# A gated backbone layer on one core: fp32 state products become three fp32r passes, norm weights move into later copies, and the order of tasks changes

## The chip, the cores and the metric

The kernel runs on one core of one Trainium2 chip. The metric is the device time of one execution of the program on that core, in microseconds, and the median over the runs counts.

## The reference, cut to what matters

One layer, 1024 latent tokens behind 256 context tokens, width 1024. One input projection feeds two branches: a bidirectional chunked gated linear attention (GLA, 4 heads, keys of 128, values of 256) and a differential attention (8 heads, values of 128). Each branch is normalised, weighted per channel, gated, projected; the two are merged by gates and projected once more.

```python
h  = modulate(x, shift, scale); hc = modulate(ctx, ...)      # RMSNorm, adaLN
gq, gk, gv, gg, lr, dq, dk, dv, dg, mg, md = split(h @ w_in) # and of hc
# GLA, per head and direction; cum is the running sum of log_a in a chunk
scores  = (q * exp(cum - ref)) @ (k * exp(ref - cum)).T
o_intra = tril(scores) @ v
k_state = k * exp(last - cum)
s = decay * s + k_state.T @ v             # the state, chunk after chunk
o = o_intra + (q * exp(cum)) @ s          # forward plus backward
# differential attention, per head
a = softmax(q1 @ k1.T) - lam * softmax(q2 @ k2.T);  od = a @ vd
# merge
A = rms_norm(o)  * gla_norm                  * silu(gg)
B = rms_norm(od) * diff_norm * (1 - lam_init) * silu(dg)
y = sigmoid(mg) * (A @ w_br_gla) + sigmoid(md) * (B @ w_br_diff)
out = x + g_x * (y @ w_out)
```

All inputs and outputs are float32. `gla_norm` has 256 entries, one per value channel of a head, and `diff_norm` has 128.

## The kernel before, in words

**How it is written.** A scheduler in the program (`Driver`) writes out the instruction streams of all engines. Each piece of work is a Python generator, a task, started by `spawn(task, at, prio)`. The scheduler keeps its own clock, which follows TensorE's planned time, and of the tasks that are due it lets the one with the smallest `prio` number issue its next instructions. A task gives way with `yield`: for an event, for a planned time, or with `yield d.on("ACT", *tiles)` until the planned time at which the tiles are ready and ACT's planned queue has room. `acq(tag)` waits for a buffer of a pool and `rel(tag, at)` gives it back. So priorities, events and pool sizes set the order in which instructions stand on each engine. Once written, each engine runs its stream in order, and a semaphore wait of one instruction holds everything behind it on that engine. Most engine instructions go through one helper and carry line L201; matrix multiplications carry L349, transposes L375. In the profile they are told apart by the names of their tiles.

**Two kinds of matmul.** `mm` on float32 operands is one fp32 instruction, which leaves two records in the profile. `mm3` takes operands split into an upper half `hi` and a remainder `lo`, both of type fp32r, and adds up three fp32r matmuls: hi x hi, hi x lo, lo x hi. `split` makes the two halves: ACT copies to `hi`, and DVE subtracts `hi` from the source to give `lo`.

**The stages, in order of time.**

- 0 to 80 us: the prologue. The adaLN vectors, the normalised tokens, transposed into the blocks `hk` (context) and the `h` tiles, and the low-rank decay inputs.
- 80 to 176 us: the projections `gk` and `gq`. Within them `job_la` computes the log decays `g` for all heads on ACT (Exp, then Ln, which need another activation table) and stores them; `job_gate` makes sums of tokens (`gb` steps on DVE).
- 176 to 519 us: four pairs of projections, each 1024 channels, by a scheme with seven products (`BY7`, in the order `gv`, `dv`, `dg`, `gg`). Sums of weights are formed ahead (`sums`), stored to `d_s` and read back. `gv` are the GLA values, stored to `d_v` as float32; `dv` the values of the attention, stored to `d_dv` as two halves; `dg` and `gg` are the two gates, finished as SiLU by `post_gate` or `direct`, which end with a multiplication on POOL by the norm weights (`gdif`, 128x512, or `ggla`).
- 520 to 910 us: the remaining projections (keys and queries of the attention, merge gates) on TensorE, and between their matmuls the four GLA heads.
- 910 to 1455 us: the attention, 64 units of 128 queries of one head, with the projection by `w_br_gla` (`mb`) as filler between its matmuls. `att_order` lists the turns: scores `S`, transposes `T`, at @ values `A`. `AHEAD0` units of scores come first, and then scores run `LEAD` units ahead.
- To 1626 us: the projection by `w_br_diff`, the merge, the output projection.

**One GLA head** (function `gla`). `prep` loads keys and decays and forms their running sums. `kstates(0)` and `kstates(1)`, for the two directions, go through five groups of two 128-token blocks: load the values `gv` by DMA, exponential `ge` on ACT, product with the keys on POOL, two transposes on TensorE into the psum tile `gt`, copy to `gkt` on ACT. `products` multiplies `gkt` by `gv`, two fp32 matmuls per group into psum `gt`, and `upd` on DVE adds them to the decayed state: `gsb` in `bwd`, `gsf` in `fstates`. `intra` forms the scores from factors of queries and keys, masks them on POOL (`gsc`) and adds the two directions on DVE (`gso`). `forward` adds up, per group, six matmuls into psum `go`: for each of the two blocks, queries by forward state, queries by backward state, scores by values. `post` normalises, multiplies by the gate and transposes (`tp<-ident,gp`); ACT and DVE split the transposed result into two halves `pl`, which are stored to `d_aT`. In the attention, `att_fin` transposes likewise (`b1`), and ACT copies the result to `bb`, which is stored to `d_bT`.

The line that starts a direction's group of products, and the one that adds scores by values:

```python
en = self.mm(pu[:, j], kt[:, j], v[:, j], True, True)        # products
en = self.mm(po[:, j], sc[:, j], v[:, j], False, True)       # forward
```

Of the kernel before, what the change touches and what calls it, by code (L numbers as in the profile page):

```python
# [232 lines left out]
class Hybrid:  # L233
# [10 lines left out]
        gk=("sbA2", 1), gla=("sbA2", 2), gq=("sbA2", 1), gsb=("sbA2", 8), gsf=("sbA2", 4), ge=("sbA2", 2),  # L244
        gkt0=("sbA2", 2), gkt1=("sbA2", 2), gqe=("sbA2", 4), gqr=("sbA2", 1), gkk=("sbA2", 1),
        gsc=("sbA2", 1), gso=("sbA2", 2), gp=("sbA2", 2), gj=("sbA2", 1), gv0=("sbA2", 2), gv1=("sbA2", 2),
# [157 lines left out]
    def scratch(self):  # L404
# [4 lines left out]
        self.d_v = [d(f"d_v{c}", [T, 512]) for c in range(2)]  # L409
# [46 lines left out]
    def consts_late(self):  # L456
# [9 lines left out]
        self.ggla = self.c("ggla", [P, 256])  # L466
        self.dma(self.ggla, bc(a["gla_norm"][0], 256))
        self.gdif = self.c("gdif", [P, P])
        self.dma(self.gdif, bc(a["diff_norm"][0], P))
# [10 lines left out]
        self.pool.tensor_scalar(self.ggla, self.ggla, 0.5, 0.0, ALU.mult, ALU.add)  # L480
        self.pool.tensor_scalar(self.gdif, self.gdif, 1.0 - LAM_INIT, 0.5, ALU.mult, ALU.mult)
# [348 lines left out]
    def phase_a(self):  # L830
# [8 lines left out]
        self.gla_done, self.gla_free, self.gla_back, self.gla_intra, self.gla_sf = (  # L839
            [Event() for _ in range(4)] for _ in range(5))  # L840
# [29 lines left out]
        self.ev_pl, self.ev_pw, self.ev_zl = Event(), Event(), Event()  # L870
# [36 lines left out]
    BY7 = (("gv", C_GV), ("dv", C_DV), ("dg", C_DG), ("gg", C_GG))  # L907
# [35 lines left out]
    def pair_weights(self, cols, ev_load, ev_run):  # L943
# [54 lines left out]
        def run():  # L998
            yield ev_run
            for g in range(len(cols)):  # L1000
# [23 lines left out]
                for n, o in (("t1", "w22"), ("t3", "w12"), ("t4", "w21"), ("v22", "v22")):  # L1024
                    for k in range(4):
# [71 lines left out]
    def pairs(self, wp):  # L1097
# [3 lines left out]
        def loads():  # L1101
# [7 lines left out]
            for g, (what, _) in enumerate(self.BY7):  # L1109
                w = 512 if what in ("dg", "gg") else 640  # L1110
                for n in self.SUMS:
                    for k in range(4):
# [5 lines left out]
                        d.set(ev_z[g, n, k], d.when(z))  # L1118
                        if (g, n, k) == (len(self.BY7) - 1, "s4", 1):
                            d.set(self.ev_zl)  # L1120
# [27 lines left out]
        for g, (what, _) in enumerate(self.BY7):  # L1148
# [5 lines left out]
            def out(g, r, c, t, x, tag):  # L1154
# [3 lines left out]
                if what in ("dg", "gg"):  # L1158
# [6 lines left out]
                    yield e  # L1165
                    gain, dst, w = (self.gdif, self.d_dg, P) if what == "dg" else (self.ggla, self.d_gg, 256)
# [1635 lines left out]
```

## Time and profile before

| what | value |
|---|---|
| median of 3 runs | 1622.63 us (1622.59 to 1624.02) |
| time of the profiled execution | 1627.62 us |
| its span; mean granted TensorE clock | 1625.9 us; 0.996 |
| TensorE matmul / weight load (PE / PEld) busy | 98% / 82% |
| VectorE (DVE) / ScalarE (ACT) / GpSimd (POOL) busy | 75% / 51% / 39% |
| moved by DMA | 331.16 MB, mean 204 GB/s |

How to read the views: a group of instructions has a line number, an engine, an operation and its tiles as output<-inputs, a shape and a count, then busy time and mean duration, then the idle time in front of them and what ended it. "128x512" is partitions by elements. The chain that ended last is followed backwards from the last instruction; a matmul counts in it only until the next one takes over. The windows view gives for a stretch of time each engine's busy time, and behind them the granted clock as a share of full speed, the share of time that the DMA engines were busy, and GB/s.

### The profile page before, as it was taken

To read this page: it belongs to the slowest core of one execution; us is meant where nothing else is said; L and a number is where in the kernel's file an instruction comes from. 1 tells how busy PE (TensorE), PEld (TensorE's weight loads), DVE (VectorE), ACT (ScalarE), POOL (GpSimd) and SP (SyncE) were. 2 spreads that over 40 slices of the span, in tenths; PEclk is the share of its full clock that TensorE was granted. 3 is DMA by queue.
4 is the path that set the end of the run, shared out by engine and by line. 5 is a ranking of instruction groups with operands and counts; after the bars stand their busy time and mean duration, and the time that the engine had idled before them with its cause. 6 is when DMAs were issued, how large, how long until landed. Compare 5 with 4: busy or idle time off the path is not lost.

```text
span 1625.9 us, 24368 instructions
## 1 busy us (share of the span) xinstructions
PE 1597.1 (98%) x8229; PEld 1331.9 (82%) x8229; DVE 1226.6 (75%) x2117; ACT 836.2 (51%) x1719; POOL 635.6 (39%) x663
## 2 busy tenths in 40 slices
PE   7999999999999999999999999999999999999999
PEld 2687888888788888888888878888888888888887
DVE  4776955467677778867677687888887888888994
ACT  4756633435343354546445466665665655656431
POOL 1400000001314657544555066666665666660000
PEclk9999999999999999999999999999999999999999
DMA  8666798887867558574535854545588455348662
GB/s 295 221 237 233 267 345 312 272 311 272 302 200 264 171 163 251 161 227 133 174 116 153 224 155 128 139 119 157 147 261 243 141 140 161 111 144 292 199 205 103
DMA packets 259565, 331.16 MB, mean 204 GB/s; under 512 B 22600, under 2 KB 160752, under 8 KB 259440
## 3 DMA queue, kind: packets, MB, share of 16 engines
q1 hardware_dynamic: 259440, 329.60, 63.6%
q8 instruction: 65, 1.06, 0.3%
q14 instruction: 60, 0.49, 0.1%
HBM read 225.20 MB, written 104.33 MB: 203 GB/s over the span
## 4 chain that ended last, share of the span: by engine, by line
PE 88%; DVE 5%; DMA 2%; ACT 2%; POOL 1%; issue 1%; SPq 0%; ACTq 0%; DVEq 0%; POOLq 0%
PE mm L349 30%; PE mb L349 10%; PE s L349 8%; PE mc L349 7%; PE b L349 6%; PE tp L349 6%; PE gt L349 5%; PE b L375 4%; PE gs L349 4%; PE go L349 4%; PE mz L349 2%; DVE sm L201 2%; PE tp L375 2%; POOL at L201 1%; DMA w<-in_w_ada 1%
## 5 line engine op out<-in xcount | busy, mean ns | idle before, releaser
L349 PE MATMUL mm<-w,h 128*128 128x512 f32 x912 | 231.0, 400 | 0.0
L349 PE MATMUL mb<-h,wt 128*128 128x512 f32 x840 | 223.8, 401 | 0.0
L201 DVE TENSOR_REDUCE sm<-s 128x1 f32<-128x1024 f32 (+1 forms) x192 | 193.1, 1035 | 10.2 <-PE s L349 4.3
L201 ACT ACTIVATE e<-s,sm 128x1280 f32<-128x1280 f32 x128 | 169.4, 1329 | 56.4 <-DVE sm L201 55.6
L349 PEld LDWEIGHTS mm<-w,h 128*128 128x128 f32 x912 | 167.4, 188 | 32.7
L201 POOL TENSOR_TENSOR at<-ac,at 128x512 fp32r<-128x512 f32 x128 | 187.1, 1462 | 10.7
L349 PE MATMUL mm<-h,w 128*128 128x512 f32 x672 | 173.8, 409 | 3.5 <-ACT p L201 3.4
L201 POOL TENSOR_SCALAR at<-ac 128x512 fp32r<-128x512 f32 x128 | 100.4, 784 | 189.1 <-ACT ac L201 188.9
L349 PEld LDWEIGHTS mb<-h,wt 128*128 128x128 f32 x840 | 151.0, 188 | 28.2 <-DVE ft L201 0.3
L349 PE MATMUL s<-hk,aq 128*128 128x512 f32 x744 | 169.4, 364 | 2.1 <-ACT e L201 2.0
L349 PEld LDWEIGHTS mm<-h,w 128*128 128x128 f32 x672 | 127.1, 193 | 31.1 <-ACT p L201 3.8
L201 DVE TENSOR_TENSOR w<-raw,w 128x512 fp32r<-128x512 f32 x128 | 96.3, 770 | 52.6 <-ACT w L201 51.6
L349 PEld LDWEIGHTS s<-hk,aq 128*128 128x128 f32 x744 | 118.0, 189 | 20.6 <-ACT e L201 5.5
L349 PE MATMUL b<-at,vv 128*128 128x256 f32 x960 | 130.1, 287 | 1.1 <-ACT ac L201 0.8
L349 PEld LDWEIGHTS b<-at,vv 128*128 128x128 f32 x960 | 119.6, 191 | 2.7 <-ACT ac L201 1.0
L201 ACT ACTIVATE ac<-b 128x512 f32<-128x512 f32 x122 | 72.4, 597 | 94.3 <-PE b L375 94.1
L201 DVE SCALAR_TENSOR_TENSOR e<-e,sm,e 128x1280 f32<-128x1280 f32 x64 | 120.0, 1876 | 0.9
L201 POOL TENSOR_TENSOR sm<-sm,nhalf 128x2 f32<-128x2 f32 (+2 forms) x94 | 109.2, 1162 | 27.6 <-DVE sm L201 22.3
L201 ACT ACTIVATE w<-raw 128x512 fp32r<-128x512 f32 x128 | 77.8, 625 | 77.7 <-PE tp L349 21.1
L349 PE MATMUL mm<-w,g 128*128 128x512 f32 x432 | 105.7, 389 | 0.0
L201 POOL TENSOR_TENSOR p<-p,gdif 128x512 f32<-128x512 f32 x12 | 17.4, 1458 | 198.9 <-DVE p L201 174.2
L349 PEld LDWEIGHTS mm<-w,g 128*128 128x128 f32 x432 | 81.1, 188 | 16.8
(353 smaller groups left out, 3125.2 us busy)
## 6 DMA issues: line engine op xcount, KB each, us to landing
raw<-in_w_in SPq DMA_DIRECT2D x62, 512.0 KB, 4.4
g<-d_s SPq DMA_DIRECT2D x32, 640.0 KB, 6.5
g<-d_s SPq DMA_DIRECT2D x32, 512.0 KB, 6.0
aq<-d_qT SPq DMA_DIRECT2D x124, 128.0 KB, 3.6
d_dv<-pl SPq DMA_DIRECT2D x40, 256.0 KB, 3.5
gv<-d_v SPq DMA_DIRECT2D x40, 256.0 KB, 3.3
d_kT<-pl SPq DMA_DIRECT2D x40, 256.0 KB, 2.9
hk<-d_kT SPq DMA_DIRECT2D x32, 320.0 KB, 6.1
```

Source lines behind the costliest of these rows:

```text
L201: self.ins = f(out, *args, **kw).ins
L349: self.ins = self.nc.tensor.matmul(out, lhsT, rhs, start=start, stop=stop, skip_group_check=more).ins
L375: self.nc.tensor.transpose(out, src, self.ident[:n, :n])
```

## The change

It has three parts.

1. **Products in three passes.** The 72 state products and the 32 products of scores by values go from one fp32 matmul each to `mm3`. For that `gkt`, `gv` and `gso` hold two fp32r halves: ACT copies the upper half, a subtraction on DVE makes the lower. `d_v` is stored as two halves (40 stores of them), and each group loads both (80 loads of `gv` for 40). The products take psum tile `tp` in place of `gt`. The pools `gkt0`, `gkt1`, `gv1`, `gso` and `gp` shrink from two buffers to one, and the queries come in four loads of 256 columns into two buffers, by a new task `queries`, in place of one load of 1024.
2. **Norm weights.** The 32 multiplications of gates by norm weights on POOL are gone. The weights are held as one column per 128 channels (`gcol`) and applied where the channels lie on partitions: in the copies behind the GLA heads' last transposes (ACT's copy takes `scale=gcol`, DVE's subtraction becomes multiply and subtract), and in ACT's copy of `att_fin`.
3. **Order.** The pairs come as `dv`, `dg`, `gv`, `gg`. Priorities change (see the diff); `job_la` yields between its Exp and its Ln; one load of weights in the first pair waits for an event (`ev_z1`); the second rope table is made in the third pair instead of the first; the attention begins with two units of scores instead of three, and for the first turns runs three units ahead instead of four.

The diff, cut to its core:

```diff
-        gk=("sbA2", 1), gla=("sbA2", 2), gq=("sbA2", 1), ...
-        gkt0=("sbA2", 2), gkt1=("sbA2", 2), ...
-        gsc=("sbA2", 1), gso=("sbA2", 2), gp=("sbA2", 2), ... gv0=("sbA2", 2), gv1=("sbA2", 2),
+        gk=("sbA2", 1), gla=("sbA2", 2), gq=("sbA2", 2), ...
+        gkt0=("sbA2", 1), gkt1=("sbA2", 1), ...
+        gsc=("sbA2", 1), gso=("sbA2", 1), gp=("sbA2", 1), ... gv0=("sbA2", 2), gv1=("sbA2", 1),
...
-        d.spawn(self.job_lr(), prio=8)
-        d.spawn(self.job_la(), prio=3)
+        d.spawn(self.job_lr(), prio=1)
+        d.spawn(self.job_la(), prio=2)
         d.spawn(self.consts_late(), At(105.0), prio=2)
-        d.spawn(self.job_gate(), At(70.0), prio=2)
-        d.spawn(self.sums(), prio=3)
+        d.spawn(self.job_gate(), At(70.0), prio=4)
+        d.spawn(self.sums(), prio=2)
...
-    BY7 = (("gv", C_GV), ("dv", C_DV), ("dg", C_DG), ("gg", C_GG))
+    BY7 = (("dv", C_DV), ("dg", C_DG), ("gv", C_GV), ("gg", C_GG))
...
+                    if (g, n, kk) == (0, "v22", 0):
+                        yield self.ev_z1
...
-                            if g == 0:
+                            if g == 2:
                                 d.spawn(self.rope_tables(1), prio=2)
...
                 for j in range(2):
                     self.act.activation(ex[j], ex[j], AF.Exp, scale=-1.0)
+                yield self.d.on("ACT", *ex)
                 for j in range(2):
                     self.act.activation(ex[j], ex[j], AF.Ln, bias=1.0)
...
-        self.pool.tensor_tensor(tv, tv, g.unsqueeze(1).to_broadcast([P, n, w]), ALU.mult)
...
-            d.spawn(kstates(0), prio=2)
-            d.spawn(intra(), prio=3)
+            d.spawn(kstates(0), prio=-1)
+            d.spawn(intra(), prio=-1)
...
-                kt = self.t(f"gkt{e}", [P, 2, P])
-                v = self.t(f"gv{e}", [P, 2, 256])
-                self.dma(v, self.d_v[h // 2][g * 256:(g + 1) * 256, cols].rearrange("(c p) e -> p c e", p=P))
+                kt = self.t(f"gkt{e}", [P, 2, 2, P], F32R)
+                v = self.t(f"gv{e}", [P, 2, 2, 256], F32R)
+                for x in range(2):
+                    self.dma(v[:, x], self.d_v[x][h // 2][g * 256:(g + 1) * 256, cols].rearrange("(c p) e -> p c e", p=P))
...
-                en = self.act.activation(kt, pt, AF.Copy)
+                yield self.act.activation(kt[:, 0], pt, AF.Copy)
+                en = self.dve.tensor_tensor(kt[:, 1], pt, kt[:, 0].bitcast(F32), ALU.subtract)
...
-            yield from self.acq("gt")
-            pu = self.t("gt", [P, 2, 256])
+            yield from self.acq("tp")
+            pu = self.t("tp", [P, 2, 256])
             for j in js:
-                en = self.mm(pu[:, j], kt[:, j], v[:, j], True, True)
+                en = self.mm3(pu[:, j], kt[:, 0, j], kt[:, 1, j], v[:, 0, j], v[:, 1, j], True, True)
+            self.rel(f"gkt{e}", en)
...
-                    d.spawn(factors(e, g, qr, kr, ev[e]), prio=3)
+                    d.spawn(factors(e, g, qr, kr, ev[e]), prio=-1)
...
-                sc = self.t("gso", [P, 2, P])
-                en = self.dve.tensor_tensor(sc.rearrange("p j (s t) -> p j s t", t=64), raw[:, :, :, 0], raw[:, :, :, 1],
-                                            ALU.add)
+                sc = self.t("gso", [P, 2, 2, P], F32R)
...
+                yield self.act.activation(hi, x, AF.Copy)
+                en = self.dve.tensor_tensor(lo, x, hi.bitcast(F32), ALU.subtract)
...
-                    en = self.mm(po[:, j], sc[:, j], v[:, j], False, True)
+                    en = self.mm3(po[:, j], sc[:, 0, j], sc[:, 1, j], v[:, 0, j], v[:, 1, j], False, True)
...
-            e = yield from self.split(pt.rearrange("p x c t -> p x (c t)"), hi, lo)
+            for x in range(2):
+                e = self.act.activation(hi[:, x], pv[:, x], AF.Identity, scale=self.gcol[:, x:x + 1])
+            yield e
+            for x in range(2):
+                e = self.dve.scalar_tensor_tensor(lo[:, x], pv[:, x], self.gcol[:, x:x + 1], hi[:, x].bitcast(F32), ALU.mult,
+                                                  ALU.subtract)
...
-        d.spawn(kstates(1), prio=2)
+        d.spawn(kstates(1), prio=-1)
+        d.spawn(queries(), prio=2)
...
-    LEAD, AHEAD0 = 4, 3
+    LEAD, AHEAD0 = 4, 2
...
+            lead = self.LEAD if o >= 3 else self.LEAD - 1
...
-        self.rel("b1", self.act.activation(bb, pb, AF.Copy))
+        self.rel("b1", self.act.activation(bb, pb, AF.Identity, scale=self.gcol[:, 2:3]))
```

How the instruction streams move is shown at three places. First TensorE, at the first group of state products of the first GLA head, between matmuls of a projection (`mm`). Before:

```order
2243 L349 MATMUL mm_4856<-w_4554,h_62_356 128x512
2244 L349 MATMUL mm_4856<-w_4583,h_64_358 128x512
2245 L349 MATMUL mm_4856<-w_4584,h_64_358 128x512
2246 L349 MATMUL mm_4856<-w_4583,h_65_359 128x512
2247 L349 MATMUL gt_4876<-gv_926_4823,gkt_925_4822 128x256 x2
2248 L349 MATMUL mm_4856<-w_4612,h_69_373 128x512
2249 L349 MATMUL mm_4856<-w_4613,h_69_373 128x512
2250 L349 MATMUL mm_4856<-w_4612,h_70_374 128x512
```

And now:

```order
2264 L349 MATMUL mm_4908<-w_4742,h_146_625 128x512
2265 L349 MATMUL mm_4908<-w_4741,h_147_626 128x512
2266 L349 MATMUL tp_4977<-gv_972_4928,gkt_971_4927 128x256 x6
2267 L349 MATMUL mm_4989<-w_4630,h_170_732 128x512
2268 L349 MATMUL mm_4989<-w_4631,h_170_732 128x512
2269 L349 MATMUL mm_4989<-w_4630,h_171_733 128x512
2270 L349 MATMUL mm_4989<-w_4659,h_180_778 128x512
2271 L349 MATMUL mm_4989<-w_4660,h_180_778 128x512
```

Two fp32 matmuls into `gt` have become six fp32r matmuls into `tp`, at the same kind of place.

Second ACT, where `job_la` works beside the projection `gk`: `w` is a converted weight, `raw` the loaded one, `g` the log decays (Exp first, then, behind the table load, Ln), `p<-mm` the copy that frees a psum bank of the projection. Before:

```order
114 L201 ACTIVATE w_1367<-raw_1293 128x512
115 L201 ACTIVATE w_1371<-raw_1293 128x512
116 L201 ACTIVATE g_266_1278<-g_266_1278 128x1280
117 L201 ACTIVATE g_280_1327<-g_280_1327 128x1280
118 L201 ACT_TABLE_LOAD
119 L201 ACTIVATE g_266_1278<-g_266_1278 128x1280
120 L201 ACTIVATE g_280_1327<-g_280_1327 128x1280
121 L201 ACTIVATE p_1379<-mm_1250 128x512
122 L201 ACTIVATE p_1381<-mm_1251 128x512
```

And now:

```order
113 L201 ACTIVATE w_1329<-raw_646 128x512
114 L201 ACTIVATE g_266_1281<-g_266_1281 128x1280
115 L201 ACTIVATE g_276_1317<-g_276_1317 128x1280
116 L201 ACTIVATE w_1362<-raw_1276 128x512
117 L201 ACTIVATE p_1366<-mm_1242 128x512
118 L201 ACTIVATE p_1368<-mm_1243 128x512
119 L201 ACTIVATE w_1379<-raw_1276 128x512
120 L201 ACT_TABLE_LOAD
121 L201 ACTIVATE g_266_1281<-g_266_1281 128x1280
122 L201 ACTIVATE g_276_1317<-g_276_1317 128x1280
123 L201 ACTIVATE w_1412<-raw_1360 128x512
```

The two Exp have moved ahead of the conversions from the next `raw` tile, and the first of those conversions and the two bank copies have moved between the Exp and the table load.

Third DVE, where the GLA heads end and the attention begins: `wt` is the lower half of a weight of `w_br_gla`, `pl<-tp` the lower half of a GLA output, `sm` the maxima of the first unit's scores. Before:

```order
1000 L201 TENSOR_TENSOR pl_8782<-tp_8776,pl_8781 128x512
1001 L201 TENSOR_TENSOR wt_8809<-raw_8461,wt_8808 128x1024
1002 L201 TENSOR_REDUCE sm_8826<-s_1795_8824 128x1
1003 L201 TENSOR_REDUCE sm_8825<-s_1795_8824 128x2
1004 L201 TENSOR_REDUCE sm_8827<-s_1795_8824 128x1
1005 L201 TENSOR_SCALAR sm_8826<-sm_8826,sm_8825 128x1
1006 L201 TENSOR_SCALAR sm_8827<-sm_8827,sm_8825 128x1
1007 L201 TENSOR_TENSOR wt_8811<-raw_8555,wt_8810 128x1024
1008 L201 TENSOR_REDUCE sm_8845<-s_1795_8824 128x1
1009 L201 RECIPROCAL sm_8915<-sm_8828 128x1
```

And now:

```order
1076 L201 SCALAR_TENSOR_TENSOR pl_9098<-tp_9090,gcol,pl_9097 128x256 x2
1077 L201 TENSOR_TENSOR wt_9132<-raw_9037,wt_9131 128x1024
1078 L201 TENSOR_TENSOR pl_9180<-tp_9174,pl_9179 128x512
1079 L201 TENSOR_TENSOR wt_9154<-raw_9101,wt_9153 128x1024
1080 L201 TENSOR_TENSOR pl_9214<-tp_9208,pl_9213 128x512
1081 L201 TENSOR_REDUCE sm_9278<-s_1849_9276 128x1
1082 L201 TENSOR_REDUCE sm_9277<-s_1849_9276 128x2
1083 L201 TENSOR_REDUCE sm_9279<-s_1849_9276 128x1
1084 L201 TENSOR_SCALAR sm_9278<-sm_9278,sm_9277 128x1
1085 L201 TENSOR_SCALAR sm_9279<-sm_9279,sm_9277 128x1
```

Both first weight splits and the last GLA output now stand ahead of the first maximum; before, one split stood behind the first unit's first maxima.

More of the change, by code (lines that the diff above doesn't have):

```diff
@@ L408, in scratch @@
         self.d_la = [[d(f"d_la{r}{h}", [P, T]) for h in range(4)] for r in range(2)]
-        self.d_v = [d(f"d_v{c}", [T, 512]) for c in range(2)]
+        self.d_v = [[d(f"d_v{j}{c}", [T, 512]) for c in range(2)] for j in range(2)]
         self.d_gg = [d(f"d_gg{c}", [S, 512]) for c in range(2)]
@@ L1253, in direct @@
             return
-        if self.BY7[g][0] == "gv":
-            yield from self.acq("p")
-            x = self.t("p", [P, 512])
-            self.rel(tag, self.act.activation(x, pm, AF.Copy))
-            self.store([(self.d_v[1][o:o + P], x)], ("p", 1))
-            return
         yield from self.acq("p")
@@ L1642, in backward, with queries @@
                         self.rel("gsb", d.now)
-                self.rel("gt", en)
-                self.rel("gkt1", d.now)
+                self.rel("tp", en)
                 self.rel("gv1", d.now)
                 yield AtPE(en)
+        def queries():
+            if h:
+                yield self.gla_q[h - 1]
+            for g in range(1, 5):
+                yield from self.acq("gq")
+                q = st["q", g] = self.t("gq", [P, 2, P])
+                self.dma(q, self.d_q[h][:, (g - 1) * 256:g * 256].rearrange("p (c t) -> p c t", t=P))
+                d.set(ev_ql[g], d.when(q))
+            d.set(self.gla_q[h])
         def factors(e, g, qr, kr, ev):
@@ L1759, in fstates @@
                         self.rel("gsf", d.now)
-                self.rel("gt", en)
+                self.rel("tp", en)
                 if g == 0:
-                    self.rel("gkt0", d.now)
                     self.rel("gv0", d.now)
```

69 lines of the change are left out of this document (32 added, 37 removed).

## The prediction

> **What bounds the kernel now.** I read the page first: which engine is busy, and who owns the chain that ended last.
>
> ```profile
> PE 1597.1 (98%) x8229; PEld 1331.9 (82%) x8229; DVE 1226.6 (75%) x2117; ACT 836.2 (51%) x1719; POOL 635.6 (39%) x663
> ...
> PE 88%; DVE 5%; DMA 2%; ACT 2%; POOL 1%; issue 1%; SPq 0%; ACTq 0%; DVEq 0%; POOLq 0%
> ```
>
> TensorE works 98% of the span and owns 88% of the chain. So two things can change the time: microseconds of matmul that go or come, and the few places where TensorE stands still. The waits of TensorE, longest first, name those places; I keep the four that the change touches.
>
> ```profile
> PE mm L349 <- ACT p L201: 3.4, 1, 3.4
> ...
> PE s L349 <- ACT e L201: 2.0, 2, 1.8
> PE tp L349 <- DMA g<-d_s: 1.7, 1, 1.7
> ...
> PE mm L349 <- DVE hk L201: 0.7, 1, 0.7
> ```
>
> In the windows, the stage in which the GLA heads run beside the late projections reads so (columns: length, then busy time and count of PE, PEld, DVE, ACT, POOL, then granted clock, DMA share, GB/s):
>
> ```profile
> 530.00:900.00 370.00, 369.95 (x1872) 311.58 (x1871) 278.91 (x528) 181.90 (x494) 205.31 (x256) 1.00 0.58 172
> ```
>
> TensorE stands still for 0.05 us of 370 there. A matmul microsecond removed in this stage is one off the span, as long as the helpers stay hidden.
>
> **The change, part by part.** The sum is made against the profiled execution's own 1627.62 us; the median of the timed runs, 1622.63, lies 5.0 lower.
>
> *Products in three passes.* The chain that ended last gives the pace of each form, since it counts a matmul only until the next one takes over (columns: start, us, what).
>
> ```profile
> 538.25 0.86 PE gt L349 x4
> ...
> 586.59 2.59 PE go L349 x12
> ...
> 964.46 2.16 PE b L349 x18
> ```
>
> An fp32 matmul of 256 columns leaves two records: 0.86 us for 4 records is two state products, 2.59 us for 12 is six matmuls, so 0.43 us each both times. The fp32r matmul of the same shape in the attention (at @ values, weights reloaded for each) takes 2.16/18 = 0.120; three passes are 0.36. There are 18 state products per head (9 each way), 72 in all, and 8 products of scores and values per head, 32 in all: 104 x (0.432 - 0.360) = 7.5 us less. Bounds: the groups of that attention matmul as a whole, gaps included, and of its weight loads:
>
> ```profile
> L349 PE MATMUL b<-at,vv 128*128 128x256 f32 x960 | 130.1, 287 | 1.1 <-ACT ac L201 0.8
> L349 PEld LDWEIGHTS b<-at,vv 128*128 128x128 f32 x960 | 119.6, 191 | 2.7 <-ACT ac L201 1.0
> ```
>
> 130.1/960 = 0.136 would leave 104 x (0.432 - 0.407) = 2.6 us, and 119.6/960 = 0.125 of weight load 6.0. I take 7.5, since 18 in a row ran at 0.120.
>
> *What the passes add beside TensorE.* 40 subtractions on DVE for the lower halves of the keys, 16 for those of the scores, 16 copies on ACT, and twice the loads of values (80 for 40) on SP. The single buffers gkt0, gkt1 and gv1 make each group's steps one behind the other:
>
> ```profile
> L201 ACT ACTIVATE gkt<-gt 128x256 f32<-128x256 f32 x40 | 15.2, 381 | 23.2 <-PE gt L375 23.2
> L201 DVE TENSOR_TENSOR gso<-gsc 128x256 f32<-128x256 f32 x16 | 9.7, 608 | 6.3 <-POOL gsc L201 6.3
> L201 POOL TENSOR_TENSOR ge<-hk,ge 128x256 f32<-128x256 f32 x20 | 17.3, 864 | 9.2 <-ACT ge L201 8.7 <-DMA gv<-d_v 0.4
> ...
> gv<-d_v SPq DMA_DIRECT2D x40, 256.0 KB, 3.3
> ```
>
> Load 3.3, the exponential priced as the copy 0.4, POOL 0.9, copy 0.4, subtraction 0.6, products 0.7: 6.3 us a group. There are 20 groups each way in 370 us, one every 18.5. So 12 us of cover are left, and the added DVE work, 56 x 0.6 = 34 us, lifts DVE from 279 to 313 of 370. I cost these at 1.0 us of new small waits; the ends are 0 and 5 (0.13 for each of 40 groups).
>
> *The wait at 126 us.* This is the largest one, and the chain shows how it comes about:
>
> ```profile
> 115.28 6.22 DMA raw<-in_w_in
> ...
> 121.57 1.15 ACT w L201 x2
> 122.73 2.33 ACT g L201 x2
> ...
> 127.55 1.25 ACT g L201
> 128.80 0.49 ACT p L201
> ...
> 129.34 2.08 PE mm L349 x4
> ```
>
> ACT stands in front of a weight conversion until its load lands at 121.5, then does two Exp, changes its table, does two Ln, and only then copies out the `mm` bank for which TensorE has waited since 125.9 (129.34 less the 3.4 of its row). In the new order the two Exp stand ahead of that conversion and the two bank copies right behind it, ahead of the table change; `yield ... on("ACT", *ex)` in `job_la` opens that gap. With the load landing at 121.5 as now, and one conversion of 0.6 and two copies of 0.5 behind it, the banks are free at 123.1, 2.8 us before TensorE asks. The wait goes, and what is late next is the lower half of the second conversion, which the same matmul stream takes only at its last step. The wait has a second price, in the windows:
>
> ```profile
> 129.34:135.00 5.66, 5.66 (x13) 4.46 (x14) 5.59 (x9) 1.44 (x3) 0.00 (x0) 0.50 0.93 342
> 135.00:141.00 6.00, 6.00 (x28) 4.90 (x27) 3.54 (x5) 1.85 (x3) 0.00 (x0) 1.00 0.66 230
> ```
>
> Right behind it the granted clock is 0.50 for 5.66 us, with 13 matmuls where the next 6.00 us hold 28: half of 5.66, 2.8 us, is lost. The two make 6.2. [...] The execution profiled is 5.0 us slower than the median, and nothing says where; if all 5.0 lay here, only 1.2 could be won in the timed runs. I take 4.7, nearer the upper end, because the wait and the slow clock have rows of their own.
>
> *The wait at 79 us.* Gate sums on DVE stood between the context's blocks, from the chain:
>
> ```profile
> 76.53 0.61 DVE hk L201
> 77.14 0.80 DVE gb L201
> 77.95 0.87 DVE hk L201 x2
> ...
> 78.94 0.74 DVE gb L201
> 79.68 0.54 DVE hk L201
> ```
>
> `job_gate` goes behind, and of four `gb` steps among the last ten blocks one is left. The 0.7 us of the wait goes; TensorE can't win more there, as its own work follows.
>
> *The start of the attention.* Rows of the timeline, TensorE first, then DVE and ACT (start, us, engine, group, idle before):
>
> ```profile
> 944.11 2.97 PE L349 MATMUL s<-hk,aq 128*128 128x512 f32 x12 [1.82 <-ACT e L201]
> ...
> 916.44 1.21 DVE L201 TENSOR_TENSOR wt<-raw,wt 128x1024 fp32r<-128x1024 f32 x1
> ...
> 938.34 2.40 DVE L201 SCALAR_TENSOR_TENSOR e<-e,sm,e 128x1280 f32<-128x1280 f32 x1
> ...
> 942.63 1.33 ACT L201 ACTIVATE e<-s,sm 128x1280 f32<-128x1280 f32 x1 [1.32 <-DVE sm L201]
> ```
>
> Scores wait for ACT's exponentials, which wait for DVE's maxima, which stand behind the mixing (2.40) and, earlier, a weight split (1.21). The new order finishes the GLA heads before the last `mg` matmuls, so that both first weight splits stand ahead of the first maximum, and it starts with two units of scores instead of three. That takes one split and one unit's reductions from DVE before the point where TensorE stalled. I take 1.5 of the 2.0; ends 3 won and 2 lost, as fewer scores ahead also means that a late mix is felt sooner.
>
> *Cost nothing.* The 32 gate multiplications on POOL go:
>
> ```profile
> L201 POOL TENSOR_TENSOR p<-p,gdif 128x512 f32<-128x512 f32 x12 | 17.4, 1458 | 198.9 <-DVE p L201 174.2
> ```
>
> They took 1.46 us each, but a gate is stored hundreds of microseconds before it is read, and TensorE never waited for one. The scaled copies that take the weights over read one more operand per partition; they run under matmuls, as the rows above show ACT at half load. `dv` is now the first of the pair jobs and `gv` the third, and both write two halves; DVE subtracts 20 times more (0.6 each, 12 us) in stages of 90 us. The 1.7 us wait for `g<-d_s` came in the `dg` job, where each left-hand tile serves four token tiles instead of five; `dg` is second now, with the same stores of weight sums between the loads. I move the wait and leave its size.
>
> *Sum.* 7.5 + 4.7 + 0.7 + 1.5 - 1.0 = 13.4 less. On the profiled execution that is 1614.2 in the same state of things; on the median, 1622.6 - 13.4 = 1609.2 us.
>
> **Rivals.** (a) *The clock is spared anyway, or the wait stays.* If the timed runs don't pay the wait, or a load landing 3 us later keeps it, 4.7 goes: 1609.2 + 4.7 = 1613.9. For it: the 5.0 us between profile and median. Against: ACT's order alone frees the banks. Chance 0.2. (b) *The passes don't do what they say*: at 0.136 a pass they win 2.6 instead of 7.5, and the time is 1614.1. Against: 18 in a row at 0.120. Chance 0.06. (c) *A new wait of some 2 us in the second pair job or the GLA stage with a half clock behind it*: 2 + 2.8, so 1614.0; a wait of 1.7 us is there now without it, for `g<-d_s`. Chance 0.08. (d) *Slower*: the state chains become the bound. In-order TensorE meets each product with its lower half, or its values, not yet there. It decides from 13.4/40 = 0.34 us a group on; at 0.5 us for each of 40 groups the time is 1609.2 + 20 = 1629. For it: single buffers, an SP queue with 80 loads where a late one holds the next, DVE at 85%. Against: 6.3 us of steps in 18.5, and the chains end some 84 matmuls before the stage does. Chance 0.06. My forecast, 1609, has the remaining 0.6.
>
> **How the numbers follow.** From 1622.6, everything won fully (7.5 + 6.2 + 0.7 + 3) gives 1605.2. At the other end (a), (b) or (c) alone gives about 1614, and one of them with the attention's start 2 us worse instead of 1.5 better gives 1617.5. What lies outside is mostly (d). The range is 1604 to 1617.5. A measurement here tells 0.2%, 3.2 us, from no change. Faster by more: all of my own case, most of (a) to (c): 0.89. Within: two of (a) to (c) together: 0.05. Slower: (d): 0.06.
>
> **What would show it.** Right: the chain has `tp<-gv,gkt` six for two products at 0.72 us, the group of `go` at 4 x 0.432 + 6 x 0.120 = 2.45 us instead of 2.59; no wait of `mm` for ACT at 126 us and a granted clock of 1.00 in 125 to 150; only one stretch of half clock left, near 50 us; first scores of the attention some 12 us earlier. Wrong: PE's waits name `gkt`, `gv` or `gso`; the GLA stage holds more than a few us of idle TensorE; three passes take over 0.40.

## The result: slower by 0.3%, where 0.8% faster was forecast

The changed kernel takes 1628.8 us (median of 6 runs, 1626.1 to 1630.2), the kernel before 1623.3 in the same runs (1621.3 to 1626.4). The ratio is 1.003, interval 1.0018 to 1.0041. The forecast was 1609.2 with a range up to 1617.5.

The page of the changed kernel, the same rows as before:

```profile
PE 1599.2 (98%) x8333; PEld 1328.7 (82%) x8333; DVE 1248.3 (77%) x2209; ACT 858.4 (53%) x1771; POOL 581.7 (36%) x631
...
PE 85%; DVE 5%; ACT 3%; POOL 2%; issue 2%; DMA 2%; SPq 0%; ACTq 0%; POOLq 0%; DVEq 0%
```

TensorE was to lose 7.5 us of busy time, and it has 2.1 more. From the chain that ended last, the group of two state products and one of `go`:

```profile
537.54 0.72 PE tp L349 x6
...
581.95 2.43 PE go L349 x14
```

Six passes take 0.72 us and the `go` group 2.43, as forecast (0.72, 2.45). So the passes do what they say, and other matmuls have become dearer. The waits of TensorE, in all and then in 520 to 905 us alone:

```profile
...
PE mc L349 <- DVE aq L201: 1.0, 1, 1.0
...
PE s L349 <- ACT e L201: 0.4, 1, 0.4
```

```profile
PE tp L375 <- POOL p L201: 1.4, 1, 1.4
PE gt L375 <- DVE gkt L201: 1.2, 2, 1.0
PE s L349 <- ACT p L201: 0.7, 1, 0.7
PE tp L349 <- DMA gv<-d_v: 0.7, 2, 0.5
PE gt L375 <- POOL ge L201: 0.7, 2, 0.5
```

And the windows of the GLA stage and of the stretch around 126 us:

```profile
530.00:900.00 370.00, 365.98 (x1989) 312.51 (x1988) 306.44 (x601) 195.90 (x532) 199.95 (x257) 1.00 0.68 205
125.00:150.00 25.00, 25.00 (x113) 20.60 (x111) 15.67 (x24) 15.17 (x22) 0.00 (x0) 1.00 0.65 235
```

The waits at 79 and 126 us and the half clock behind the second are gone, and so is the 1.7 us for `g<-d_s`. The GLA stage has 4.0 us of idle TensorE where it had 0.05. Behind two of its waits, 1.4 and 1.0 us long, the granted clock is halved for 3.41 us. Behind the same two waits in a_edge, a run of the experiments below with the same order of instructions, the clock stays full:

```profile
817.80:821.10 3.30, 3.30 (x10) 2.67 (x10) 3.30 (x6) 0.57 (x2) 1.80 (x2) 0.50 0.60 152
```

```profile
811.10:814.40 3.30, 3.30 (x16) 2.55 (x17) 3.30 (x5) 0.98 (x2) 1.89 (x2) 1.00 0.56 163
```

That is 1.7 us lost in the profiled execution of the changed kernel. Together with the idle time these losses are 5.7 us, less than the 6.9 us that the waits at 79 and 126 us and their half clock took before, so they don't make the kernel slower. What does is seen where one form is compared with itself. From the groups by form, a projection in the pairs and one at the end of the kernel, first before, then after (busy time, mean ns of one):

```profile
L349 PE MATMUL mm<-w,g 128*128 128x512 f32 x432 | 105.7, 389 | 0.0
L349 PE MATMUL mc<-h,ya 128*128 128x512 f32 x144 | 33.1, 389 | 0.0
L349 PE MATMUL mz<-h,wt 128*128 128x512 f32 x48 | 11.2, 389 | 0.0
```

```profile
L349 PE MATMUL mm<-w,g 128*128 128x512 f32 x432 | 108.9, 396 | 0.0
L349 PE MATMUL mc<-h,ya 128*128 128x512 f32 x144 | 33.1, 389 | 0.0
L349 PE MATMUL mz<-h,wt 128*128 128x512 f32 x48 | 11.5, 395 | 0.0
```

The same matmul, with the same tiles at no wait, is 6 to 7 ns longer in two forms and not in the third. Counted from one start to the next in the trace, `mm<-w,g` goes from 226.7 to 233.3 ns. Summed over all 512-column matmuls that follow one of the same line within 300 ns, the excess over 226.7 was 7.5 us before and is 17.5 now. That is 10.0 us in a place where the prediction had no term.

The forms that got slower take their weights from a tile on one side of the core's memory and their rows from the other (`w`, `h`, `ya` lie on the left, `g`, `wt` on the right). The new constant `gcol` takes 32 bytes in each partition where `ggla` and `gdif` took 1536. Before, weights and rows started alike modulo 128 bytes in all but 46 of the 5194 matmuls of 512 columns; with the change the left side moved by 32, and 2570 of them have weights and rows that start 32 bytes apart (counted from the addresses of the built programs). Not all of these lose 6.6 ns. Two large forms among them already stood above 226.7 before, and lose less: `mb<-h,wt` goes from 229.9 to 232.8 ns, the scores `s<-hk,aq` from 231.4 to 232.7. So the sum is 10 us and not 17.

### The profile page after: what moved, and what is told of

It reads as the page before. It is cut to its first block, busy times and chain, and to the rows that moved or that the text cites. A ratio compares the mean times of both kernels' runs of the same rounds, so it can differ in the third digit from the quotient of the medians.

```text
span 1627.8 us, 24787 instructions
## 1 busy us (share of the span) xinstructions
PE 1599.2 (98%) x8333; PEld 1328.7 (82%) x8333; DVE 1248.3 (77%) x2209; ACT 858.4 (53%) x1771; POOL 581.7 (36%) x631
## 4 chain that ended last, share of the span: by engine, by line
PE 85%; DVE 5%; ACT 3%; POOL 2%; issue 2%; DMA 2%; SPq 0%; ACTq 0%; POOLq 0%; DVEq 0%
PE mm L349 30%; PE mb L349 9%; PE tp L349 7%; PE s L349 7%; PE mc L349 7%; PE b L349 6%; PE gs L349 4%; PE go L349 4%; PE b L375 4%; PE gt L349 3%; DVE sm L201 2%; PE mz L349 2%; PE tp L375 2%; ACT e L201 1%; POOL at L201 1%
## 5 line engine op out<-in xcount | busy, mean ns | idle before, releaser
L349 PE MATMUL mm<-w,h 128*128 128x512 f32 x912 | 227.6, 398 | 0.0
L201 POOL TENSOR_TENSOR at<-ac,at 128x512 fp32r<-128x512 f32 x128 | 188.8, 1475 | 10.7
L201 POOL TENSOR_SCALAR at<-ac 128x512 fp32r<-128x512 f32 x128 | 96.8, 756 | 194.7 <-ACT ac L201 194.5
L349 PE MATMUL mm<-h,w 128*128 128x512 f32 x672 | 165.4, 398 | 0.3 <-DVE h L201 0.3
L201 DVE TENSOR_TENSOR w<-raw,w 128x512 fp32r<-128x512 f32 x128 | 89.3, 720 | 54.6 <-ACT w L201 54.2
L201 ACT ACTIVATE p<-mm 128x512 f32<-128x512 f32 (+1 forms) x104 | 60.2, 586 | 69.1 <-PE mm L349 54.3
```

Of the source, the lines that this page charges most:

```text
L201: self.ins = f(out, *args, **kw).ins
L349: self.ins = self.nc.tensor.matmul(out, lhsT, rhs, start=start, stop=stop, skip_group_check=more).ins
```

## The experiments

**Is it the start of the tiles?** Three kernels whose instructions stand in the same order as their model's, and one with nothing but matmuls.

```diff
a_pad:   -        self.gcol = self.c("gcol", [P, 3])
         +        self.gcol = self.c("gcol", [P, 11])
a_edge (the changed kernel), b_edge (the kernel before):
         -    EDGE = 96
         +    EDGE = 64
```

> The changed kernel with gcol 44 bytes wide instead of 12, so that every tile on the left side of the on-chip memory moves up by 32 bytes and nothing else changes: every engine's instructions stand in the same order. In the changed kernel the tiles on the left start at 32 modulo 64 bytes and those on the right at 0; before, both start at 0. Its trace shows 512-column matmuls with weights from the one side and rows from the other at 233 ns from start to start (mm<-w,g 233.3, mz<-h,wt 233.1), those with both from one side at 226.7 (mc<-h,ya, mz<-h,yb), where before all of these took 226.7. Summed over all 512-column matmuls, the excess over 226.7 ns is 17.5 us now and 7.5 us before. Theory (different start modulo 64 slows the pair): all at 226.7, excess near 7.5, time 1628.8 - 10 = 1618.8. Rival (the pace comes from the new order or from more DMA traffic): 233 stays, 1628.8.

> The changed kernel with the filler at the start of the right side (EDGE) at 64 bytes instead of 96, so that tiles on both sides start at 32 modulo 64. Same order on every engine. Theory (only the difference between the two starts counts): 226.7 ns everywhere, 1618.8. Rival (a start off a multiple of 64 bytes is slow by itself): the matmuls within one side, at 226.7 now, stay there although both start at 32, so this rival can only mean rows or weights from the right side; mm<-w,g stays at 233 and the time at 1628.8 or above.

> The kernel before with EDGE at 64 bytes instead of 96: left side at 0, right side at 32 modulo 64, same order on every engine. Theory: mm<-w,g and its kind go from 226.7 to 233 ns, and the kernel before becomes about 10 us slower, 1633. Rival (the slow pace belongs to the new order): no change, 1623.3.

> Not the layer: twelve rows of 40 fp32r matmuls alone, weights and rows from two tiles that start at a multiple of 64 bytes, with offsets in bytes by line (weights, rows): (0,0), (0,32), (32,0), (32,32), (0,64), (64,32), (0,16), (16,16), (0,4), (0,96), and with 256 columns (0,0), (0,32). The two weights of a row lie 768 bytes apart. Theory: the step from start to start is 226.7 ns for (0,0), (32,32) and (0,64), and 233 for (0,32), (32,0), (64,32) and (0,96); at 256 columns a few ns as well. Rival (the slow pace needs other engines' traffic): 226.7 in all.

Measured: a_edge 1618.3 us (ratio to before 0.9966, 0.9952 to 0.9979), b_edge 1633.3 (1.0053, 1.0039 to 1.0068), a_pad 1623.2 (0.9994, 0.9985 to 1.0004). The row of `mm<-w,g` in a_edge, b_edge and a_pad:

```profile
L349 PE MATMUL mm<-w,g 128*128 128x512 f32 x432 | 106.1, 390 | 0.0
```

```profile
L349 PE MATMUL mm<-w,g 128*128 128x512 f32 x432 | 108.5, 395 | 0.0
```

```profile
L349 PE MATMUL mm<-w,g 128*128 128x512 f32 x432 | 107.1, 392 | 0.0
```

32 bytes, and no instruction moved, make the changed kernel 10.5 us faster and the kernel before 10 us slower. In a_edge both sides start at 32 modulo 64 and the pace is the old one (mean 390 ns, 389 before), so the difference between the two starts counts. a_pad was expected at 1618.8 and missed by 4.4 us. There the sides start 64 bytes apart, and the step is 229.0 ns where the weights start at 0 and the rows at 64. The other way round, rows at 0 and weights at 64, it is 233.3 (`mc<-wt,h`, 48 matmuls). The kernel of matmuls alone shows the same middle value. From its groups by form, (0,0) is L15, (0,32) L17, (32,0) L19, (32,32) L21, (0,64) L23, (64,32) L25, (0,16) L27, (16,16) L29, (0,4) L31, (0,96) L33:

```profile
L31 PE MATMUL ps<-x,w 128*128 128x512 f32 x40 | 9.6, 398 | 0.0
L17 PE MATMUL ps<-x,w 128*128 128x512 f32 x40 | 9.5, 395 | 0.0
L25 PE MATMUL ps<-x,w 128*128 128x512 f32 x40 | 9.5, 396 | 0.0
L33 PE MATMUL ps<-x,w 128*128 128x512 f32 x40 | 9.5, 395 | 0.0
L19 PE MATMUL ps<-x,w 128*128 128x512 f32 x40 | 9.5, 395 | 0.0
L27 PE MATMUL ps<-x,w 128*128 128x512 f32 x40 | 9.4, 394 | 0.0
L29 PE MATMUL ps<-x,w 128*128 128x512 f32 x40 | 9.4, 391 | 0.0
L23 PE MATMUL ps<-x,w 128*128 128x512 f32 x40 | 9.3, 391 | 0.0
L21 PE MATMUL ps<-x,w 128*128 128x512 f32 x40 | 9.3, 390 | 0.0
L15 PE MATMUL ps<-x,w 128*128 128x512 f32 x40 | 9.2, 389 | 0.0
```

From start to start: 226.7 ns at (0,0), 227.3 at (32,32), 228.9 at (0,64), 233.4 at (0,32), 233.2 at (32,0), 233.3 at (0,96) and at (64,32), 231.8 at (0,16), 236.3 at (0,4). At (16,16), where both start alike too, it is 230.0: equal starts are enough at 0 and 32, not at 16. In these rows no other engine works (ACT is idle for the 118.4 us up to the end of L35, DVE and POOL have no instruction there) and the kernel issues no DMA, so the loss needs no one else's traffic. What makes it, no run shows. At 256 columns there was no loss (119.9 at (0,0), 117.9 at (0,32)), where a few ns were expected, and (0,64) was expected at 226.7.

With tiles alike, the change is 5.5 us faster than before. The forecast was 13.4. The rest of the runs looks for the missing 8.

**One part alone, on the kernel before.** Here and below, tiles start alike modulo 128 bytes in every kernel.

```diff
b_front: only job_lr 1, job_la 2, job_gate 4, sums 2, and yield self.d.on("ACT", *ex)
b_pass:  only the first part (mm3, halves, pools, queries), old priorities
b_norm:  only the second part (gcol), with EDGE = 64
```

> The kernel before with the new order of the first 180 us alone: the four priorities (job_lr 1, job_la 2, job_gate 4, sums 2) and the yield between Exp and Ln of job_la. In the profiled executions the stage from the first gk matmul to the first pair is 8.2 us shorter with the change (147.2 before, 139.0 with it and EDGE 64), of which 6.9 are the waits at 79 and 126 us and the half clock. Theory of the prediction: the timed runs gain 5.4 of it, 1618. Rival (the execution profiled before had more of that wait than the timed ones, being 4 us slower than their median): about 1 to 2, 1622.

> The kernel before with the first part of the change alone: state products and scores by values in three fp32r passes, with all that they need (pools, loads by halves, queries in four pieces, products in psum tile tp), in the old order and with the old priorities; all tiles still start alike modulo 128 bytes. In the changed kernel with EDGE 64 the GLA stage, from the last matmul of the pairs to the first scores of the attention, takes 387.9 us against 391.3 before, with 4.2 us of TensorE standing still in it (1.4 for POOL p, 1.2 for DVE gkt, 0.7 for ACT p, 0.6 for POOL ge). Theory (passes bring 7.5, waits in that stage take back 4): 1623.7 - 3.5 = 1620. Rival (the waits come from the new priorities, not from the passes): 1623.7 - 7.5 = 1616.

> The kernel before with the norm weights alone moved into the copies behind the last transposes, and EDGE at 64 so that tiles on both sides start alike modulo 128 bytes in spite of the smaller constants. Theory of the prediction (costs nothing): 1623.7, same. Rival (the copies by halves, two instructions of 256 columns in place of one of 512 on ACT and DVE, delay DVE's queue in the GLA stage): slower by a few us, and PE's waits in 520 to 905 us name DVE.

b_front takes 1618.1 us against 1623.6 (0.9972, 0.9961 to 0.9984): 5.5 faster, the 5.4 of the prediction, so the timed runs did pay for the two waits. b_pass takes 1636.7 (1.0082, 1.007 to 1.0095), outside what either theory gave, and b_norm 1643.6 (1.0128, 1.0114 to 1.0142), where "same" was expected. The waits of TensorE in b_pass, 520 to 920 us, then the longest one in the timeline, TensorE and DVE:

```profile
PE tp L349 <- DVE gkt L201: 6.2, 2, 4.0
...
```

```profile
675.34 0.40 PE L349 MATMUL tp<-gv,gkt 128*128 128x256 f32 x2
679.76 0.58 PE L349 MATMUL tp<-gv,gkt 128*128 128x256 f32 x1 [4.03 <-DVE gkt L201]
```

```profile
673.96 0.68 DVE L201 TENSOR_REDUCE sm<-p 128x8 f32<-128x512 f32 x1
...
678.32 1.07 DVE L201 TENSOR_TENSOR_SCAN gla<-fresh,gla 128x258 f32<-128x258 f32 x1
679.32 0.39 DVE L201 TENSOR_TENSOR gkt<-gt,gkt 128x256 fp32r<-128x256 f32 x1
```

Two passes are through and the third needs the lower half of the keys, which stands behind other tasks' work on DVE. That is the mechanism of rival (d), in the old order; it makes 6.2 of the 9.2 us that TensorE stands idle in this stage. b_norm has its waits elsewhere in that stage, from the same list:

```profile
PE tp L375 <- POOL p L201: 3.6, 1, 3.6
PE mm L349 <- DVE w L201: 3.3, 1, 3.3
PE gs L349 <- DVE gkk L201: 1.0, 1, 1.0
...
```

These waits are not the whole price. In both kernels the clock halves behind them, as it did behind the two waits of the changed kernel: at 678.1, 821.5 and 951.2 us of b_pass, and at 674.6, 889.7 and 954.5 us of b_norm, for 3.41 or 6.83 us each. In the windows of b_norm the granted clock is 0.96 in 640 to 680 us, 0.91 in 880 to 920 and 0.96 in 920 to 960; in b_pass it is 0.98 over 520 to 905 us and 0.995 over the whole span. At 0.50 the matmuls `mm<-h,w` of the kernel before start 427 ns apart, at 1.00 227 (medians). From these two numbers I estimate that half of the time that TensorE works at 0.50 is lost, in the GLA stage 5.3 us of b_pass and 4.7 of b_norm. The table below sets this out for every kernel.

**One part left out, of the changed kernel.**

```diff
a_gprio:  -prio=-1 of kstates, intra, factors   +prio=2, 3, 3      (EDGE = 64)
a_fp32:   without the first part                                   (EDGE = 64)
a_nonorm: without the second part                                  (EDGE = 96)
a_lead:   AHEAD0 = 3, LEAD = 4 throughout                          (EDGE = 64)
b_fpg:    the kernel before, with the first part, the GLA priorities and b_front
```

> The changed kernel with EDGE 64 and the old priorities of the GLA tasks (kstates 2, intra and factors 3). Theory (with them the single buffers stall the products, as in b_pass, where the GLA stage took 399.3 us for 387.9): 1618.3 + 11 = 1629, with PE's waits for DVE gkt. Rival (the priorities matter little once the norm multiplications are off POOL): 1618.3.

> The changed kernel with EDGE 64 and without its first part: state products and scores by values are single fp32 matmuls as before, with their old pools and loads; priorities, norm weights and order as changed. Theory (104 x 0.072 = 7.5 us of matmul come back, 4.2 us of waits in the GLA stage go): 1618.3 + 3.3 = 1621.6. Rival (the waits have nothing to do with the passes): 1618.3 + 7.5 = 1625.8. Third (single fp32 products under the new priorities stall as the parts did alone): above 1628.

> The changed kernel without its second part: the gates are multiplied by the norm weights on POOL as before, the copies behind the last transposes are plain, and the constants have their old size, so that tiles start alike modulo 128 bytes with EDGE 96. From the first scores on, the matmuls' excess over their quiet pace (226.7, 120, 109 ns) sums to 34.4 us before, 34.1 in b_front, 35.0 in b_pass, but 39.9 in b_norm and 38.9 in the changed kernel with EDGE 64. Theory (the scaled copies cost the attention 5 us): about 33 there, 1618.3 - 5.5 = 1613. Rival of the prediction (they cost nothing): 1618.3.

> The changed kernel with EDGE 64 and the attention's turns as before (AHEAD0 = 3, LEAD = 4 throughout). With EDGE 64 alone the stretch from the first scores to the end is 715.9 us against 711.0 before, with the same matmuls in it. Theory (two units of scores ahead cost later what they save at the start): about 4 us less, 1614. Theory of the prediction (the shorter lead saves 1.5): 1620. Third (the loss comes from the order of the tail and of the fills, which the lead doesn't set): no change, 1618.3.

> The kernel before with the passes, the new GLA priorities (-1) and the new order of the first 180 us, without the norm weights, the pairs' order and the attention's turns. Passes with the old priorities made it 13.2 us slower (b_pass), the first 180 us alone 5.5 faster (b_front). Theory (passes and priorities belong together: -7.5 and 4 back in waits): 1618.1 - 3.5 = 1614.6. Rival (the passes lose by themselves, and something else in the change makes up for it): above 1620.

| kernel | us | ratio to before | GLA stage | TensorE idle in it | lost to the half clock | left | from the first scores on |
|---|---|---|---|---|---|---|---|
| before (profiled execution) | | | 391.3 | 0.3 | 0 | 391.0 | 711.0 |
| b_norm | 1643.6 | 1.0128 | 408.0 | 11.3 | 4.7 | 392.0 | 717.3 |
| a_fp32 | 1624.0 | 1.0008 (0.9997 to 1.0018) | 394.1 | 2.5 | 0 | 391.5 | 717.4 |
| b_pass | 1636.7 | 1.0082 | 399.3 | 9.2 | 5.3 | 384.8 | 711.6 |
| a_edge | 1618.3 | 0.9966 (0.9952 to 0.9979) | 387.9 | 4.2 | 0 | 383.7 | 715.9 |
| a_gprio | 1627.8 | 1.0032 (1.0020 to 1.0045) | 397.1 | 9.5 | 1.6 | 386.0 | 717.5 |
| a_nonorm | 1621.6 | 0.9994 (0.9984 to 1.0004) | 395.5 | 8.2 | 2.8 | 384.6 | 710.1 |
| a_lead | 1618.1 | 0.9967 (0.9956 to 0.9978) | 389.7 | 4.4 | 1.7 | 383.6 | 715.6 |
| b_fpg | 1625.3 | 1.0019 (1.0010 to 1.0028) | 395.6 | 8.3 | 2.7 | 384.6 | 711.1 |

(The GLA stage runs from the last matmul of the pairs to the first scores; the last column ends with the last matmul. The stage and its parts are from the records of the profiled executions, in us. "Lost to the half clock" is an estimate: half of the time in which TensorE worked at a granted clock of 0.50, from the 427 and 227 ns above.)

The column "left" separates the two kinds of kernel. With fp32 products it is 391.0 to 392.0 us, with the passes 383.6 to 386.0. So the passes win 6.2 us (b_pass against before) to 7.8 (a_edge against a_fp32), where 7.5 were forecast, and what they or the norm part cost in this stage is idle time and the half clock behind it. In the timed runs of the finished order the priorities are worth 9.5 us by the medians and 10.7 by the ratios, the passes 5.7 and 6.8. a_fp32 was expected at 1621.6 or 1625.8 and lies between the two.

The time of a_gprio is the forecast one, but not for the reason given. Its waits in 520 to 920 us:

```profile
PE tp L375 <- DVE gp L201: 4.8, 2, 4.1
PE gs L349 <- DVE gkk L201: 2.0, 1, 2.0
PE tp L349 <- DVE gkt L201: 1.0, 2, 0.6
...
```

Only 1.0 us is for the keys `gkt`. With the old priorities the last head ends so late that its last transposes stand right in front of the first scores of the attention, where a_edge has 92 matmul records between them. So the 4.1 us wait for `gp` finds no projection to hide behind.

b_fpg missed its 1614.6 by 10. The two kernels without the norm part, b_fpg and a_nonorm, have the same long GLA stage (395.6 and 395.5 us), so it seems that passes and priorities need the norm part as well; what in it makes the difference wasn't tried. The attention's turns are worth nothing (a_lead). And a_nonorm tells where 5 us went: without the norm part the stretch from the first scores on is 5.8 us shorter, while the GLA stage is 7.6 us longer, so its time alone (1621.6, where 1613 was expected) would have hidden it.

**The scaled copy or the order?** In `att_fin` the scaled copy takes 0.48 us for 0.39, and the scheduler plans 0.093 more for it.

```diff
a_finfast: +        self.act.more = -0.093      # planned as a plain copy, the instruction stays scaled
a_finplan: +        self.act.more = 0.093       # planned as a scaled copy
           -  ... AF.Identity, scale=self.gcol[:, 2:3]
           +  ... AF.Copy
```

> The changed kernel with EDGE 64, and att_fin's scaled copy entered in the planner at the cost of a plain one (0.093 us less), so that the attention's order on all engines is the one that a plain copy gives; the instructions are the same. From the first scores to the end it is 715.9 us with EDGE 64 alone, 711.0 before and 710.1 without the norm part. Theory (the order that follows from the higher cost makes the waits): 710 to 711 there, 1618.3 - 5 = 1613. Rival (the copy's own 0.09 us, 32 times on ACT between transposes, makes them): 716, 1618.3.

> The changed kernel with EDGE 64 and a plain copy in att_fin, entered in the planner at the scaled copy's cost, so that every engine's instructions stand in the same order as with EDGE 64 alone; the norm weights of the differential branch are left out. Theory (the order makes the waits): 716 us from the first scores to the end, 1618.3. Rival (the copy's own time): 711, 1613.

a_finfast takes 1614.7 us (0.9947, 0.9934 to 0.9959) and 710.4 from the first scores on; a_finplan 1618.4 (0.9979, 0.9969 to 0.9989) and 715.8. The waits of TensorE in 1000 to 1500 us, with EDGE 64 alone and in a_finfast:

```profile
PE b L375 <- DVE b1k L201: 1.9, 4, 0.8
PE mc L349 <- DVE aq L201: 1.1, 1, 1.1
PE b L375 <- ACT b1k L201: 0.9, 2, 0.7
PE b L375 <- ACT ac L201: 0.8, 1, 0.8
PE b L349 <- ACT ac L201: 0.8, 1, 0.8
PE b L349 <- POOL at L201: 0.7, 2, 0.3
PE b L375 <- DVE at L201: 0.6, 2, 0.3
PE mb L349 <- DVE ft L201: 0.6, 1, 0.6
...
```

```profile
PE b L375 <- ACT ac L201: 1.9, 1, 1.9
PE b L375 <- DVE b1k L201: 1.2, 2, 0.7
PE mb L349 <- DVE ft L201: 0.9, 1, 0.9
PE b L349 <- POOL at L201: 0.3, 1, 0.3
```

So the copy's own 0.09 us cost nothing, as the prediction said (a_finplan, with the plain copy in the same order, is as slow as a_edge). The order that the scheduler makes of 0.09 us more costs 5.4 us of this stretch in the traces and 3.7 us in the timed runs, where 5 were expected. The 0.09 us in the plan are what the copy really takes, so this is no error of the plan: that the truer cost led to the worse order is chance. a_finfast computes all that the changed kernel does, and it is the fastest of all: 0.5% faster than before.

## Why the prediction was wrong, point by point

- **The step that failed** is "Cost nothing": it weighed the norm part by the instructions it removes and adds, and not by the 1.5 KB that leave the constants. That moved half of the tiles by 32 bytes against the other half, which costs 10.5 us (a_edge against the changed kernel, the same order). It turns 0.3% faster into 0.3% slower.
- **The same step, once more:** the scaled copy in `att_fin` was held to run under matmuls. It does (a_finplan), but its planned cost reorders the attention, 5.4 us in the traces and 3.7 in the timed runs (a_finfast).
- **Products:** the size was right. Six passes took 0.72 us and the `go` group 2.43, and without idle time and half clock the GLA stage is 6.2 to 7.8 us shorter with the passes, against 7.5 forecast. In the timed runs, with their waits, they are worth 5.7 to 6.8, against 7.5 - 1.0.
- **New waits in the GLA stage:** 1.0 forecast, with ends 0 and 5; 4.2 in a_edge's trace. The prediction counted DVE's load (313 of 370 us forecast, 306 measured) and not its queue. 1.2 us of it show how: the transposes of the next group wait for `gkt`, because the `gt` bank, which ACT's copy used to free, is now free only after DVE's subtraction. The longest wait, 1.4 us for POOL's `p`, is not explained by any run.
- **126 and 79 us:** 5.4 forecast, 5.5 measured in b_front. Rival (a) is out for the most part, and the 5.0 us between the profiled execution and the median didn't lie here alone. The half clock does stay away at times: the wait for ACT's `p` near 126 us was 3.4 us long before, with a clock of 0.50 behind it, and 2.8 in b_edge, with 0.91 in 120 to 130 us and 0.92 in 130 to 140; in b_norm and b_pass it was 3.0 and 2.7, and the clock was 1.00 in both stretches. The wait of 1.8 us for ACT's `e` was followed by the half clock in b_pass and b_norm, at 951 and 954 us (0.96 over 920 to 960 us of b_norm), and the same wait by the full clock in the kernel before (1.00 over the same 40 us).
- **Start of the attention:** the wait for ACT's exponentials fell from 2.0 to 0.4, but the turns bring nothing in the end: a_lead, with the old ones, takes 1618.1 us against 1618.3. From the first scores on, the best of the changed kernels needs 710.4 us (a_finfast) and the kernel before 711.0, so of the 1.5 forecast at most 0.6 is there.
- **`g<-d_s`:** "I move the wait and leave its size". The 1.7 us went, from 343.1 to 341.5 us for the four pairs in a_edge: a gain that wasn't forecast.
- **The rivals:** (d) gave 1629 and the time is 1628.8, but that is luck: its stalls are 4 us of 20, and the start of the tiles is 10.5. Its mechanism shows in b_pass, with the old priorities, and hardly in a_gprio (1.0 us for `gkt`). (c), a new wait of some 2 us with a half clock behind it, did come, in the GLA stage of the changed kernel's profiled execution (2.4 us of waits and 1.7 lost to the clock). For that reason the sign "only one stretch of half clock left" failed there, and in a_edge it held. (b) is out, by the 0.72 us.

On aligned tiles: forecast 13.4, measured 5.5. Of the 8 between them, by the stages of the profiled executions, 5 are the attention's order, 3 the GLA waits, 1.5 the attention's start, less the 1.7 at `d_s`. In the timed runs the order is worth 3.7 of the 5.

## What to carry to other kernels

When a change resizes or removes a buffer, compute where all later tiles start before costing any instruction: a constant of 12 bytes was dearer here than 104 rewritten matmuls were worth. Where a scheduler writes the order, a part of a change can't be priced alone (by themselves, b_pass was 13 us slower, b_norm 20 us slower and b_front 5 us faster; the whole change, on tiles that start alike, is 5 us faster), and 0.09 us in one planned cost changed the time by 4 us; so read what each engine's queue holds ahead of a new step, not how busy the engine is. Add to the price of a wait the half clock that can follow it: in b_pass 9.2 us of idle TensorE in the GLA stage brought 5.3 more. Compare one matmul form's mean duration between two traces first: it shows a change of pace that no list of waits shows (`mm<-w,g` 389 ns before, 396 after, at 0.0 us of waits).

## What the runs showed of the hardware

In micro, a 512-column fp32r matmul with its weights reloaded each time took 226.7 ns from start to start when weights and rows both started at 0 modulo 128 bytes in their partitions (L15), and 227.3 with both at 32 (L21), with no other engine at work. It took 230.0 with both at 16 (L29), 233.2 to 233.4 when they started 32 or 96 bytes apart (L17, L19, L25, L33), 231.8 at 16 apart (L27) and 236.3 at 4 (L31). With 64 bytes between them it took 228.9 with the weights at 0 (L23) and, in a_pad, 233.3 with the rows at 0 (`mc<-wt,h`). At 256 columns 32 bytes made no such loss in micro: 119.9 at (0,0) and 117.9 at (0,32). In the layer, `mm<-w,g` took 226.7 ns before and 233.3 in the changed kernel, 432 matmuls in each.

In its trace the kernel before had two stretches at a granted clock of 0.50, of 6.83 us each, from 49.7 and from 128.2 us; the changed kernel had one of 6.83 us from 49.8 us and one of 3.41 us from 817.7 us, behind waits of 1.4 and 1.0 us. In a_edge the clock was 1.00 behind the same two waits (811.1 to 814.4 us). The kernel before had waits of 1.7 us at 411 us (`g<-d_s`) and of 1.8 us at 944 us (`e`), and no half clock from 135 us to its last matmul.
